# Layer 1's modulation: from matmul steps among the mixers' work to VectorE dot products among layer 0's MLP blocks

## Chip, cores and metric

One NeuronCore of a Trainium2 chip runs the whole program. TensorE (PE) multiplies matrices, VectorE (DVE) and ScalarE (ACT) work on 128 partitions of a tile, GpSimd (POOL) adds some squares here, and the queue of SyncE (SP) issues every load. Each engine takes its instructions strictly in the order in which they stand in its queue; semaphores let them wait for one another. The metric is the time of one execution in microseconds (us).

## Reference

Two transformer blocks run on 256 tokens of 1024 features, in fp32. Only the first block is touched. It has two layers, and in each the scale, shift and gate vectors ("modulation") of the token stream x and of a context stream ctx come from two conditioning vectors c and c_ctx:

```python
silu_c, silu_cc = jax.nn.silu(c), jax.nn.silu(c_ctx)
...
for l in range(DEPTH):                       # DEPTH = 2
    mx = jnp.split((silu_c @ w_mod[l] + b_mod[l])[:, None, :], N_MOD, axis=-1)   # w_mod[l]: 1024 x 6144
    mc = jnp.split(silu_cc @ w_mod[l] + b_mod[l], N_MOD, axis=-1)
    zx = modulate(rms_norm(x, norm1_g[l]), mx[0], mx[1]) @ w_in[l]
    ...                                      # mixer: latent attention, Fourier group, convolution
    x = x + mx[2] * mixer_rest(fx, gx, attn_x, l)
    hx = modulate(rms_norm(x, norm2_g[l]), mx[3], mx[4])
    x = x + mx[5] * channel_mlp(hx, l)       # relu(h @ w_mlp1)^2 @ w_mlp2, 1024 -> 4096 -> 1024
```

The same is done for ctx with mc in layer 0. For each layer the modulation is a 2 x 1024 by 1024 x 6144 product, kept on the chip as a tile `mod` of 128 partitions x 2 streams x 48 columns. Block 2's cross-attention reads keys and values of a memory of 256 tokens, whose products (`memory()`) depend on nothing else.

## The kernel before

Features lie on partitions, tokens along the free axis (n = 512 for both streams, 256 for x alone). An fp32 product is three passes over exact parts: `wsplit` (line 582) loads a 512 KB chunk of weights into a slot `raw` (four slots, line 577), ACT casts it to the high part `wh`, DVE subtracts to get the low part `wl` (three slots each), and 24 matmuls per output block of 128 features take high x high, high x low and low x high. PE is fed block after block; each output block of 128 x 512 is one PSUM bank `mm` and is read by DVE and ACT when it is finished.

The modulation is `modulation(l)` (line 727), a generator with 24 steps per layer. A step takes two `raw` chunks of w_mod, 16 matmul instructions into the PSUM tile `md`, a copy `mrow` on ACT, four short matmuls with a selection matrix, and a DVE add with the bias into `mod`. All steps of both layers are *filler*: `weave` (line 1425) interleaves the mixer's chains (values and keys, queries, attention, Fourier, convolution, the input projection) by a model of the engines and takes a filler step when no other product could go. Layer 0's mixer takes the rest of layer 0's steps and then steps of layer 1; layer 1's mixer alternates layer 1's remaining steps with chunks of `memory()` (line 850; 16 chunks of 24 matmuls, tile `ax<-hl`), and what is left of `memory()` runs after the mixer. The step order is fixed when the program is built, and a scheduler may still move instructions of one engine past each other before the queues are written.

After each mixer comes the output projection (`wo`, 8 blocks) with `resid` (line 824): DVE adds the gated block to x, ACT squares x for the norm, and DVE and ACT prepare the *early* operand x times scale (tile `hl<-x,s`), on which the first two blocks of the MLP start before the norm is known. Then the norm itself: ACT's `y`, DVE's `q`, `q`, `y` (`rsqrt`, line 697), and for 8 feature tiles x 2 streams DVE's `tmp<-x,s,y` and ACT's and DVE's two parts `hl<-tmp,mod`. The MLP (`mlp`, line 1270) is 32 `up` blocks (`ev_mlp`: `tmp<-mm`, `hid`) and 32 `down` blocks (`x<-mm,mod,x`), in quarters of 8. All loads go through SP's one queue in order.

Of the kernel before, what the change touches and what calls it, by code (L numbers as in the profile page):

```python
# [27 lines left out]
# ------------------------------------------------------------------ layouts  # L28


def pack_w(w, kt, mc):
    """[kt*128, M] -> [M/mc, 128, mc/128 * kt * 128]: chunks that load contiguously, output block by block."""
    m = w.shape[1]
    return np.ascontiguousarray(
        w.reshape(kt, P, m // mc, mc // P, P).transpose(2, 1, 3, 0, 4).reshape(m // mc, P, kt * mc)
    )


def cols(v):
    """A vector of n*128 -> [128, n]."""  # L40
    return v.reshape(-1, P).T


def feat(a):
    """[T, D] -> [128, D/128, T]."""
    return a.T.reshape(-1, P, a.shape[0]).transpose(1, 0, 2)
# [97 lines left out]
INS = "ckv kr g0 a0 cq0 cq1 g1 a1 zf0 zf1".split()  # order of the blocks of w_in  # L144


def layout(i):
    """All device arrays, laid out; and where each small vector lies."""
# [4 lines left out]
    a["mem"] = np.ascontiguousarray(feat(i["mem_2"][0]))  # L153
    for l in range(2):
        a[f"w_mod{l}"] = np.ascontiguousarray(
            i["w_mod"][l].reshape(KD, P, 3, 2, KD, P).transpose(2, 4, 1, 0, 3, 5)).reshape(24, P, 2048)
# [64 lines left out]
# ------------------------------------------------------------------ program  # L221


TICK = 10.24 / 3  # of the PE's activity monitor, in us


class Engine:
    """An engine whose instructions the model of the core notes as they are issued."""
# [13 lines left out]
class Pool:  # L242
    """A tile pool whose slots' reuse the model notes."""
# [19 lines left out]
class Core:  # L263
    """The core, with a model of when each engine gets to what has been issued, in us.

    It serves only to choose the order in which work that does not depend on each other is traced."""
# [3 lines left out]
    TAIL = {"pe": 0.19, "dve": 0.16, "act": 0.18, "pool": 0.2, "dma": 2.0}  # until others see an end  # L270

    def __init__(self, nc):
# [3 lines left out]
        self.columns = {}  # tick of the PE's activity monitor -> columns counted  # L276
        self.used = {}    # tile -> end of its last use
        self.seen = {}    # tile -> accesses: box, end, engine, whether written
        self.last = 0.0   # the latest end since it was set to 0
        self.gaps = {k: [] for k in self.clock}  # when an engine waits, which later work may use  # L280
# [5 lines left out]
    def box(ap):  # L286
        """The first and last partition and element that an access touches."""
# [4 lines left out]
    def product(self, start, name, n, rows, cols, f32):  # L292
        """How long a product takes: the PE runs at half its rate after a tick with too few columns."""
# [28 lines left out]
    def after(self, ap):  # L322
        """When what has been issued so far has written ap."""
# [7 lines left out]
    def cooling(self):  # L331
        """Whether the PE has too few columns in this tick so far to run at its full rate in the next."""
# [3 lines left out]
    def place(self, key, ready, held):  # L336
        """When an instruction starts that could at ready: in the first gap that holds it, or behind the last."""
# [47 lines left out]
class Chain:  # L385
    """Work that is traced in steps: a generator that stops before products that wait for other engines.

    It yields the tiles that the next product waits for, nothing if that is all of the step, or a chain that has to
    end first. A chain that is mostly the DVE's (dve) goes on when the DVE has nothing else."""
# [6 lines left out]
class Squares:  # L396
    """Sums of squares over the features of tiles that come one by one: all but the last are added up on the way."""
# [1981 lines left out]
```

## Time and profile before

| | |
|---|---|
| time, median of 3 runs | 1751.02 us (1748.15 to 1751.82) |
| profiled execution: first to last instruction | 1750.8 us, at a mean granted TensorE clock of 0.962 |
| busy: PE, DVE, ACT, POOL | 1667.3, 1158.8, 853.1, 81.1 us |
| PE's busy time on `md` | 89.85 us for 48 steps |
| HBM traffic | 142 GB/s on average |

The profiled execution's span lies 0.2 us below the median of the runs, so the sums further down are made against 1750.8 us and need no correction. All instructions are issued by one helper, so the profile's line is always L238 and the tiles tell what an instruction is. The stages on the profile's clock: layer 0's mixer to 254 us (its own modulation is done at 200), its output projection to 296, norm and MLP to 654, layer 1's mixer to 821, the rest of `memory()` to 850, then layer 1's output projection, its MLP and block 2.

### The profile page before, as it was taken

The page shows a single profiled execution, that of the slowest core. Times are in us where ns is not written, and L with a number is a line of the kernel's source. Part 1 is how long each engine was busy: PE and PEld are TensorE (multiplying, and loading weights), DVE is VectorE, ACT ScalarE, POOL GpSimd, SP SyncE. Part 2 cuts the span into 40 slices and gives each one's busy share as a digit, 9 for nine tenths or more (in the row PEclk, how much of TensorE's full clock was granted, in tenths as well). Part 3 has the DMA queues.
Part 4 walks back from the last instruction along what each step waited for, and adds up shares of the span by engine and source line. Part 5 has one row for each costly group of instructions (what it writes and reads, how often), then busy time and mean ns, then how long its engine had stood idle before and what let it go on. Part 6 is the DMA issues. An engine that isn't in the chain of part 4 may idle for free.

```text
span 1750.8 us, 29987 instructions
## 1 busy us (share of the span) xinstructions
PE 1667.3 (95%) x12072; PEld 1429.8 (82%) x12072; DVE 1158.8 (66%) x2155; ACT 853.1 (49%) x1485; POOL 81.1 (5%) x74
## 2 busy tenths in 40 slices
PE   5899999999999998999999998899999999999997
PEld 3666668788888886767999997797888899999997
DVE  4686547743444366884679667787853868788864
ACT  4426764441323245466564446542334746666643
POOL 0000001000000011000100001011000001010000
PEclk8989999999999998989999998999988999999999
DMA  8743562233333335752756564332211475345553
GB/s 276 236 150 126 180 205 85 85 97 96 96 97 96 115 98 168 238 168 70 223 150 185 184 187 149 106 105 66 67 61 49 137 250 192 112 154 192 167 164 105
DMA packets 69403, 248.94 MB, mean 142 GB/s; under 512 B 7696, under 2 KB 13072, under 8 KB 65424
## 3 DMA queue, kind: packets, MB, share of 16 engines
q1 hardware_dynamic: 69264, 247.03, 44.2%
q8 instruction: 95, 1.56, 0.4%
q14 instruction: 44, 0.36, 0.1%
HBM read 242.80 MB, written 4.19 MB: 141 GB/s over the span
## 4 chain that ended last, share of the span: by engine, by line
PE 83%; DVE 8%; DMA 4%; ACT 4%; issue 1%; POOL 0%; SPq 0%; DVEq 0%; ACTq 0%
PE mm L238 63%; PE ax L238 11%; PE md L238 3%; PE sc L238 3%; PE fx L238 3%; DVE wl L238 2%; DMA raw<-w_in 1%; ACT wh L238 1%; DMA raw<-w_mod 1%; DVE tmp L238 1%; DVE y L238 1%; ACT L238 1%; DVE hl L238 1%; DMA x<-xc 0%; DVE x L238 0%
## 5 line engine op out<-in xcount | busy, mean ns | idle before, releaser
L238 PE MATMUL mm<-hl,wh 128*128 128x256 f32 (+2 forms) x3856 | 867.5, 320 | 15.0 <-DVE rw_in L238 7.6
L238 PEld LDWEIGHTS mm<-hl,wh 128*128 128x128 f32 x3856 | 645.5, 194 | 76.1 <-issue 8.7
L238 ACT CAST wh<-raw 128x1024 fp32r<-128x1024 f32 (+1 forms) x353 | 360.8, 1024 | 558.1 <-PE mm L238 434.3
L238 PE MATMUL mm<-hl,wl 128*128 128x256 f32 (+1 forms) x1928 | 613.4, 319 | 3.9 <-DVE wl L238 3.8
L238 DVE TENSOR_TENSOR wl<-raw,wh 128x1024 fp32r<-128x1024 f32 (+1 forms) x353 | 422.3, 1198 | 223.9 <-ACT wh L238 221.8
L238 PEld LDWEIGHTS mm<-hl,wl 128*128 128x128 f32 x1928 | 372.8, 193 | 30.4 <-DVE wl L238 6.8
L238 PE MATMUL mm<-y,wh 128*128 128x256 f32 x928 | 176.5, 290 | 7.1 <-DVE early L238 2.6
L238 PEld LDWEIGHTS mm<-y,wh 128*128 128x128 f32 x928 | 147.7, 194 | 10.3 <-DVE early L238 3.0
L238 PE MATMUL mm<-y,wl 128*128 128x256 f32 x464 | 133.1, 287 | 0.0
L238 DVE SCALAR_TENSOR_TENSOR x<-mm,mod,x 128x256 f32<-128x256 f32 x120 | 54.3, 480 | 117.9 <-PE mm L238 117.8
L238 POOL TENSOR_TENSOR sq<-sq,sq 128x256 f32<-128x256 f32 (+1 forms) x48 | 59.9, 1249 | 899.7 <-ACT sq L238 899.4
L238 PEld LDWEIGHTS mm<-y,wl 128*128 128x128 f32 x464 | 89.7, 193 | 0.6 <-issue 0.5
L238 PE MATMUL md<-raw,cs 128*32 128x256 f32 x768 | 62.6, 424 | 20.0 <-DMA raw<-w_mod 11.4
L238 PE MATMUL mm<-hid,wh 128*128 128x512 f32 x256 | 80.7, 397 | 0.0
L238 DVE SCALAR_TENSOR_TENSOR acc<-u,vec,acc 128x512 f32<-128x512 f32 (+1 forms) x120 | 73.2, 614 | 2.2
L238 ACT ACT_TABLE_LOAD x49 | 62.9, 1283 | 4.7 <-DMA vec<-vec 3.6
L238 PEld LDWEIGHTS md<-raw,cs 128*32 128x32 f32 x768 | 20.4, 115 | 48.6 <-issue 11.4
L238 PEld LDWEIGHTS mm<-hid,wh 128*128 128x128 f32 x256 | 48.2, 188 | 11.7
L238 PE MATMUL mm<-hid,wl 128*128 128x512 f32 x128 | 50.7, 396 | 0.0
L238 DVE TENSOR_REDUCE mx<-sc 128x1 f32<-128x512 f32 (+1 forms) x56 | 32.1, 574 | 24.5 <-PE sc L238 24.1
L238 PE MATMUL sc<-k,hl 96*128 96x512 f32 (+1 forms) x144 | 46.0, 420 | 1.4 <-ACT prob L238 1.4
L238 ACT CAST hl<-tmp 128x256 fp32r<-128x256 f32 (+1 forms) x62 | 28.7, 470 | 28.0 <-DVE tmp L238 27.8
(377 smaller groups left out, 2089.6 us busy)
## 6 DMA issues: line engine op xcount, KB each, us to landing
raw<-w_mlp SPq DMA_DIRECT2D x128, 512.0 KB, 3.6
raw<-w_mod SPq DMA_DIRECT2D x96, 512.0 KB, 4.7
raw<-w_up SPq DMA_DIRECT2D x22, 1024.0 KB, 4.9
raw<-w_gate SPq DMA_DIRECT2D x24, 512.0 KB, 3.6
raw<-w_down SPq DMA_DIRECT2D x16, 704.0 KB, 4.1
raw<-w_in SPq DMA_DIRECT2D x20, 512.0 KB, 4.7
raw<-w_o SPq DMA_DIRECT2D x16, 512.0 KB, 4.0
raw<-w_rw SPq DMA_DIRECT2D x14, 512.0 KB, 3.6
```

Source lines behind the costliest of these rows:

```text
L238: return f(out, *args, **kw)
```

## The change

Layer 0's modulation stays as it was. Layer 1's leaves TensorE: `dots()` loads w_mod[1] transposed, 128 output features on the partitions and 1024 inputs along the free axis (48 loads of 512 KB), broadcasts c and c_ctx to all partitions once (`cb`, 1 MB, ACT applies silu), and takes for each of the 48 chunks two DVE instructions that multiply and sum over the free axis. One chunk is issued after each output block of layer 0's MLP. `need_mod` takes from the same generator, and layer 1's mixer has `memory()` alone for filler.

```diff
+        a["w_mod0"] = np.ascontiguousarray(
+            i["w_mod"][0].reshape(KD, P, 3, 2, KD, P).transpose(2, 4, 1, 0, 3, 5)).reshape(24, P, 2048)
+    a["w_mod1"] = np.ascontiguousarray(i["w_mod"][1].T).reshape(48, P, D)
+    a["ccrow"] = np.ascontiguousarray(np.stack([i["c"][0], i["c_ctx"]]).reshape(1, 2 * D))
...
+    def dots(self):
+        nc = self.nc
+        pool = self.tm.tp
+        cb = pool.tile([P, 2 * D], F32, name="cb")
+        nc.sync.dma_start(cb, self.a["ccrow"].partition_broadcast(P))
+        nc.scalar.activation(cb, cb, AF.Silu)
+        mod, bm = self.mods[1], self.v("b_mod1")
+        w = [self.raw(self.a["w_mod1"][0], D)]
+        for b in range(48):
+            yield
+            if b < 47:
+                w.append(self.raw(self.a["w_mod1"][b + 1], D))
+            for i in range(2):
+                t = pool.tile([P, D], F32, tag="dot", bufs=1, name=self.nm("dot"))
+                nc.vector.tensor_tensor_reduce(t, w[b], cb[:, i * D:i * D + D], 1.0, bm[:, b:b + 1], ALU.mult, ALU.add,
+                                               accum_out=mod[:, i, b:b + 1])
+            if b % 16 == 15:
+                self.mod_done[1] = b // 16 + 1
...
     def fillers(self):
-        for m in self.mod_gen:
-            yield from m
+        yield from self.mod_gen[0]
...
-            next(self.filler.gen)
+            next(self.dot if l else self.filler.gen)
...
-            def fill():
-                gens = [self.filler.gen, self.memory()]
...
-            filler = Chain(fill(), fill=True)
+            filler = Chain(self.memory(), fill=True)
...
             hid[m] = (hi, lo)
+            if l == 0:
+                next(self.dot, None)
...
+        if l == 0:
+            self.dot = self.dots()
+            next(self.dot)
         self.mark(f"L{l}.norm2")
...
+            def evac(m, ps):
+                add(m, ps)
+                if l == 0:
+                    next(self.dot, None)
```

The scheduler does not leave the dot products where the code issues them. On DVE, at the norm behind layer 0's output projection, the queue of before holds the last weight split, the last early operand (`x_97` is the last of the eight tiles of x), and then the norm's `q`, `q`, `y` and the scaled tiles:

```order
L238 TENSOR_TENSOR wl_2777<-raw_2774,wh_2776 128x1024
L238 SCALAR_TENSOR_TENSOR hl_2560<-x_97,s_115,hl_2560 128x256 x2
L238 SCALAR_TENSOR_TENSOR q_2592<-y_2591 128x512
L238 SCALAR_TENSOR_TENSOR q_2592<-ax_2588,q_2592 128x512
L238 SCALAR_TENSOR_TENSOR y_2591<-q_2592,y_2591 128x512
L238 SCALAR_TENSOR_TENSOR tmp_2598<-x_90,s_115,y_2591 128x256 x2
```

The same place now, where a dot product is a row `ISA dot_...` and the row `ISA mod_117 128x1` behind it writes its sum:

```order
L240 SCALAR_TENSOR_TENSOR hl_2391<-x_97,s_115,hl_2391 128x256 x2
L240 ISA dot_2753,mod_117<-raw_2708,cb,vec 128x1024
L240 ISA mod_117 128x1
L240 ISA dot_2755,mod_117<-raw_2708,cb,vec 128x1024
L240 ISA mod_117 128x1
L240 SCALAR_TENSOR_TENSOR q_2428<-y_2427 128x512
L240 ISA dot_2796,mod_117<-raw_2751,cb,vec 128x1024
L240 ISA mod_117 128x1
L240 SCALAR_TENSOR_TENSOR q_2428<-ax_2424,q_2428 128x512
L240 ISA dot_2798,mod_117<-raw_2751,cb,vec 128x1024
L240 ISA mod_117 128x1
L240 SCALAR_TENSOR_TENSOR y_2427<-q_2428,y_2427 128x512
```

Four dot products stand between the last early operand and `y`, and eight more stand in the output projection ahead of it: one in each of the blocks that write `x_91` to `x_94`, two in those of `x_95` and `x_96`. The chunks that they read come through the same four `raw` slots as the other weights, and of the w_mod1 chunks the fourth, fifth and sixth (`raw_2659`, `raw_2708`, `raw_2751`) lie in one slot, so each is loaded when the dot products of the one before it are done. In SP's queue of the changed kernel they stand between loads of w_mlp:

```order
L240 DMA cb<-ccrow 128x2048
L240 DMA raw_2321<-w_o 128x1024
L240 DMA raw_2410<-w_mod 128x1024
L240 DMA raw_2412<-w_mlp 128x1024
L240 DMA raw_2418<-w_mlp 128x1024
L240 DMA raw_2600<-w_mod 128x1024
L240 DMA raw_2616<-w_mod 128x1024
L240 DMA raw_2622<-w_mlp 128x1024
L240 DMA raw_2659<-w_mod 128x1024
L240 DMA raw_2665<-w_mlp 128x1024
L240 DMA raw_2671<-w_mlp 128x1024
L240 DMA raw_2708<-w_mod 128x1024
```

No such w_mod load stood there before.

On PE, at the start of layer 1's mixer, the queue of before goes from the last product of the shifts (`ax<-sh`) over a modulation step to the sums of the key-value norm (`ax_5256`), two more pieces of modulation, and the key-value products (`mm<-wkh,hl`):

```order
L238 MATMUL ax_5137<-sh_5134,wl_5035 128x2
L238 MATMUL md<-cst_a,mrow_5208 128x2 x2
L238 MATMUL ax_5256<-sq_5254,cst_a 128x512
L238 MATMUL md<-raw_5243,cs 32x256 x4
L238 MATMUL md<-raw_5323,cs 32x256 x4
L238 MATMUL md<-cst_a,mrow_5241 128x2 x2
L238 MATMUL md<-raw_5335,cs 32x256 x4
L238 MATMUL mm_5377<-wkh_5250,hl_5025 128x512
```

Now the sums of the memory's norm (`ax_5358`) stand ahead of those of the key-value norm (`ax_5403`), and a whole chunk of memory products (`ax_5554`, 24 matmuls) ahead of the key-value products (`mm_5454`):

```order
L240 MATMUL ax_5259<-sh_5256,wl_5157 128x2
L240 MATMUL ax_5358<-sq_5336,cst_a 128x256
L240 MATMUL ax_5358<-sq_5356,cst_a 128x256
L240 MATMUL ax_5403<-sq_5401,cst_a 128x512
L240 MATMUL ax_5554<-hl_5368,wh_5450 128x256 x2
L240 MATMUL ax_5554<-hl_5368,wl_5451 128x256
...
L240 MATMUL ax_5554<-hl_5389,wh_5450 128x256 x2
L240 MATMUL ax_5554<-hl_5389,wl_5451 128x256
L240 MATMUL mm_5454<-wkh_5397,hl_5147 128x512
```

All `md` rows are gone from here on; on DVE the memory's norm (8 x `mem<-mem,vec,y`, 8 x `hl<-mem`) stands ahead of the second `q` of the key-value norm.

## Rows read from the trace of the kernel before

**Rows 1.** The page: span, and busy time of each engine.

```profile
span 1750.8 us, 29987 instructions
PE 1667.3 (95%) x12072; PEld 1429.8 (82%) x12072; DVE 1158.8 (66%) x2155; ACT 853.1 (49%) x1485; POOL 81.1 (5%) x74
```

**Rows 2.** Stretches, all engines: PE, PEld, DVE, ACT, POOL busy (count), clock, DMA, GB/s.

```profile
200.00:254.00 54.00, 53.20 (x466) 36.38 (x462) 26.00 (x68) 38.01 (x95) 0.00 (x0) 1.00 0.68 222
325.00:654.00 329.00, 328.69 (x1437) 269.89 (x1437) 153.67 (x201) 107.33 (x144) 9.09 (x8) 1.00 0.33 101
688.00:821.00 133.00, 123.04 (x897) 96.72 (x897) 97.16 (x212) 81.10 (x160) 3.12 (x3) 0.92 0.49 164
821.00:850.00 29.00, 29.00 (x243) 28.98 (x242) 12.16 (x14) 12.08 (x17) 0.00 (x0) 1.00 0.66 203
```

**Rows 3.** The same view for tile md alone: PE, PEld, DVE, ACT.

```profile
200.00:254.00 54.00, 16.59 (x204) 9.39 (x204) 1.64 (x10) 3.69 (x10) 1.00 0.68 222
654.00:688.00 34.00, 6.61 (x60) 2.98 (x60) 0.48 (x3) 1.11 (x3) 0.86 0.46 146
688.00:800.00 112.00, 20.44 (x216) 11.31 (x216) 1.95 (x12) 4.10 (x11) 0.91 0.56 188
```

**Rows 4.** DVE groups by shape: count, busy us, mean ns, idle before.

```profile
L238 DVE TENSOR_TENSOR wl<-raw,wh 128x1024 fp32r<-128x1024 f32 x321 | 393.8, 1228 | 196.4 <-ACT wh L238 194.3 <-ACT hl L238 1.2
...
L238 DVE SCALAR_TENSOR_TENSOR acc<-u,vec,acc 128x512 f32<-128x512 f32 x60 | 44.4, 749 | 1.2
...
L238 DVE TENSOR_TENSOR_SCAN s_z<-s_d,s_z 128x512 f32<-128x512 f32 x16 | 20.5, 1283 | 0.4
```

**Rows 5.** Loads of w_mlp: KB each, median us from issue to landing.

```profile
raw<-w_mlp SPq DMA_DIRECT2D x128, 512.0 KB, 3.6
```

**Rows 6.** Timeline of DVE, one output-projection block: start, length, idle before.

```profile
284.20 0.88 DVE L238 SCALAR_TENSOR_TENSOR x<-mm,mod,x 128x256 f32<-128x256 f32 x2 [1.53 <-PE mm L238]
285.06 1.23 DVE L238 TENSOR_TENSOR wl<-raw,wh 128x1024 fp32r<-128x1024 f32 x1
286.20 1.91 DVE L238 SCALAR_TENSOR_TENSOR hl<-x,s,hl 128x256 fp32r<-128x256 f32 x2
```

**Rows 7.** Timeline of DVE, layer 0's second norm.

```profile
301.66 0.69 DVE L238 SCALAR_TENSOR_TENSOR q<-y 128x512 f32<-128x512 f32 x1 [3.71 <-ACT y L238]
...
303.84 6.03 DVE L238 SCALAR_TENSOR_TENSOR tmp<-x,s,y 128x256 f32<-128x256 f32 x15
309.78 4.84 DVE L238 SCALAR_TENSOR_TENSOR hl<-tmp,mod,hl 128x256 fp32r<-128x256 f32 x12
```

**Rows 8.** Timeline of PE there.

```profile
316.27 0.50 PE L238 MATMUL mm<-hl,wl 128*128 128x512 f32 x1 [0.63 <-DVE wl L238]
```

**Rows 9.** Timeline of DVE, one up block.

```profile
342.64 1.23 DVE L238 TENSOR_TENSOR wl<-raw,wh 128x1024 fp32r<-128x1024 f32 x1 [2.01 <-ACT wh L238]
343.79 0.68 DVE L238 SCALAR_TENSOR_TENSOR tmp<-mm,tmp 128x512 f32<-128x512 f32 x1
345.15 0.69 DVE L238 TENSOR_TENSOR hid<-tmp,hid 128x512 fp32r<-128x512 f32 x1 [0.69 <-ACT hid L238]
348.08 1.23 DVE L238 TENSOR_TENSOR wl<-raw,wh 128x1024 fp32r<-128x1024 f32 x1 [2.24 <-ACT wh L238]
```

**Rows 10.** Timeline of PE, start of layer 1's mixer.

```profile
685.46 1.08 PE L238 MATMUL md<-raw,cs 128*32 128x256 f32 x8 [2.82 <-DVE mod L238]
688.05 0.79 PE L238 MATMUL mm<-wkh,hl 128*128 128x512 f32 x1 [1.51 <-ACT hl L238]
```

**Rows 11.** Timelines of POOL and of DVE there, the memory's norm.

```profile
690.13 1.38 POOL L238 TENSOR_TENSOR sq<-sq,sq 128x256 f32<-128x256 f32 x1 [0.31 <-ACT sq L238]
...
695.62 3.26 DVE L238 SCALAR_TENSOR_TENSOR mem<-mem,vec,y 128x256 f32<-128x256 f32 x8
698.80 1.43 DVE L238 TENSOR_TENSOR hl<-mem,hl 128x256 fp32r<-128x256 f32 x4
```

**Rows 12.** Stretches of 5 us there, columns as in group 2.

```profile
685.00:690.00 5.00, 3.03 (x13) 1.77 (x14) 2.96 (x5) 4.60 (x10) 4.47 (x5) 0.51 0.84 262
```

More of the change, by code (lines that the diff above doesn't have):

```diff
@@ L153, in layout @@
     a["mem"] = np.ascontiguousarray(feat(i["mem_2"][0]))
+    a["w_mod0"] = np.ascontiguousarray(
+        i["w_mod"][0].reshape(KD, P, 3, 2, KD, P).transpose(2, 4, 1, 0, 3, 5)).reshape(24, P, 2048)
+    a["w_mod1"] = np.ascontiguousarray(i["w_mod"][1].T).reshape(48, P, D)
+    a["ccrow"] = np.ascontiguousarray(np.stack([i["c"][0], i["c_ctx"]]).reshape(1, 2 * D))
     for l in range(2):
-        a[f"w_mod{l}"] = np.ascontiguousarray(
-            i["w_mod"][l].reshape(KD, P, 3, 2, KD, P).transpose(2, 4, 1, 0, 3, 5)).reshape(24, P, 2048)
         w = i["w_in"][l]
@@ L1234, in mixer @@
         if l:
-            def fill():
-                gens = [self.filler.gen, self.memory()]
-                while gens:
-                    for g in list(gens):
-                        y = next(g, self)
-                        if y is self:
-                            gens.remove(g)
-                        else:
-                            yield y
-            filler = Chain(fill(), fill=True)
+            filler = Chain(self.memory(), fill=True)
         self.weave(*chains, Chain(conv(), dve=True), Chain(ins), filler)
@@ L1315, in down @@
         def down(qd, *late):
-            self.linear(a[f"w_mlp2{l}"], KD, P, [hid[8 * qd + k] for k in range(8)], n,
-                        self.resid(mod, 5, streams, *late), range(8 * qd, 8 * qd + 8))
+            add = self.resid(mod, 5, streams, *late)
+            def evac(m, ps):
+                add(m, ps)
+                if l == 0:
+                    next(self.dot, None)
+            self.linear(a[f"w_mlp2{l}"], KD, P, [hid[8 * qd + k] for k in range(8)], n, evac, range(8 * qd, 8 * qd + 8))
         for qd in range(4):
@@ L1354, in block1 @@
             self.mods = [self.c1.tile([P, 2, 48], F32, name=f"mod{l}") for l in range(2)]
-            self.mod_gen = [self.modulation(l) for l in range(2)]
+            self.mod_gen = [self.modulation(0)]
             self.mod_done = [0, 0]
```

## The prediction

> **What bounds the kernel now.** First the page: PE is busy 1667 of 1751 us, DVE 1159 [rows 1]. Such a kernel gets shorter by work taken from PE, but only in stretches where PE is what is waited for. So next the stretches that the change touches [rows 2]. In layer 0's mixer, once its own modulation is done (200 to 254), PE has 0.8 us of idle time and ACT is busy 38 of 54 us. In the MLP (325 to 654) PE idles 0.3 of 329 us and DVE is busy 154: DVE has room, and nothing that delays PE would be hidden. In layer 1's mixer PE idles 10 of 133 us behind 688, and behind 821 it works on what is left of the memory without a gap. Then the modulation's own share of PE in these stretches [rows 3]: 16.6, 6.6 and 20.4 us. Of the 16.6, about 15% is the end of layer 0's steps, which stay; 9.5 steps, 14 us, are layer 1's.
>
> **Layer 0's mixer.** These steps are filler: they ran when no other product could go, so without them PE will partly wait. PE would be left with 53.2 - 14 = 39 us of work in the 54, ACT, without its copies (3.7 us [rows 3]), with 34. Neither can be packed without gaps, as the softmax goes back and forth between PE, DVE and ACT. The gain lies between 0 (every step stood in a wait) and 14 (none did). I take 8, a stage of 46 us with PE 85% busy, a little nearer to the work that remains, since three other chains run beside attention.
>
> **The output projection and the norm behind it.** Here the order shows twelve of the 96 dot products. Their price is not in the trace. The nearest row is the weight split, also fp32, both sources in SBUF, over the same 128x1024: 1.23 us [rows 4]. The sum is read out by a second, tiny instruction; DVE's tiny `mod` adds took 0.16 us each (1.64 for 10 [rows 3]). I take 1.35 us for both, a little overlapped; below, 1.2; above, the price of an operation that carries a running value, the scan: 1.28 us for 512 elements [rows 4], 2.4 to 2.5 us for 1024.
>
> In a block of the output projection DVE waits 1.53 us for PE [rows 6]. One dot product per block fits there; two make it 2.7 - 1.5 = 1.2 us late. To this come the loads. A chunk lands 3.6 us after its issue [rows 5], and is issued when a slot falls free. Take the blocks at 284.20 [rows 6] and every 5.44 us before and behind it, so that x is written at 262.4 (`x_91`) to 295.1 (`x_97`). Chunk 1 gets its slot when that first block's weight split ends, at 264.4, and lands at 268.1; DVE comes to it at 266.3 and waits. Chunk 2 waits likewise for the split two blocks later. Going through the blocks in this manner I get DVE late by 1.7, 1.4, 3.0, 2.7, 3.8 and 4.8 us, so that the update of `x_97` ends at 300.7 in place of 296.0. PE does not feel this by itself: split weights are two blocks ahead.
>
> Then the chain of loads in one slot: chunk 4's dot products end at 299.5, chunk 5 lands at 303.2, its two end at 305.9, the first `q` follows to 306.6; chunk 6, issued at 305.9, lands at 309.6; then dot, `q`, dot, `y`, with 0.69 us for `q` [rows 7]: 309.6 + 1.35 + 0.7 + 1.35 + 0.7 = 313.7. Before, `y` was done when the scaled tiles began, at 303.84 [rows 7]: 9.9 us late. Behind it stand 15 scaled tiles (6.0 us) and then the first low part, which PE's third product on the norm needs; it was done at 310.2 and will be at 320.2. There was no reserve: PE's wait at 316.27 [rows 8] is for a weight split behind this same DVE chain. So PE loses nearly all of the 9.9 us and a little at the next two splits, behind which two more dot products stand: 10.5 us. If DVE is not late at `x_97` it is 5; if the loads take 1 us more and do not overlap, 14. A pause also costs clock: in the 5 us in which PE was busy 3.0 the granted clock was 0.51 [rows 12], the lower of its two levels (1.2 of 2.4 GHz). I add 1 us (0 to 3). Sum: +11.5 us (5 to 17).
>
> The rest of `dots()` I count at nothing. The load of `cb` (1 MB, twice a chunk, so some 7 us) and its silu are first read by the first dot product, which waits for its chunk anyway; if that did not cover them, they would cost up to 4 us at that same place, and the chain of loads behind it would move by as much.
>
> **The MLP.** An up block has the split (1.15 us from start to start), `tmp` (0.68) and `hid` (0.69) on DVE, 2.52 us of every 5.44 [rows 9]. With two dot products it is 5.22: 96%, still inside. A down block has two updates (0.86 [rows 6]) and the split, 4.7 with the dots. The splits keep a reserve of one to two blocks, and DMA goes from 101 GB/s [rows 2] by one 512 KB chunk more per block to about 200, against 262 in another stretch [rows 12]. I take 0 (0 to 10).
>
> **Layer 1's mixer.** Behind 688 the steps' 20.4 us [rows 3] go away. `memory()` stays as filler, 29 us of it were run bare at the end [rows 2], and it can take the steps' places: I count all 20.4. But ahead of 688 the order has changed. PE's sums for the key-value norm now stand behind those of the memory's norm, and a whole memory chunk stands ahead of the key-value products. Before, the memory's last square was added on POOL until 691.5, its scaled tiles ran from 695.6 to 698.9 on DVE, and eight low parts followed, four of them in 1.43 us [rows 11], while the key-value products had begun at 688.05 [rows 10]. The memory's loads still go out behind weights of this stage, so I leave its norm where it was, within 3 us: low parts done at 703. The key-value norm's second `q`, `y`, scaling and split add 3 us (0.7 each): products at 706, 18 us later, in which PE has done one useful chunk, 24 x 29.0/243 = 2.9 us [rows 2]. The 6.6 us of steps ahead of 688 filled waits (2.82 and 1.51 us beside them [rows 10]) and gain nothing. Net: -20.4 + 18 - 2.9 = -5.3 us (-20 to +3).
>
> **The sum.** -8 + 11.5 + 0 - 5.3 = -1.8 us on 1750.8: 1749.0 us; the span lies 0.2 us under the median of the runs, which changes nothing. A change below 0.2% (3.5 us) cannot be told from none here, so I forecast no measurable change, out of three terms of both signs that are each larger than that.
>
> **Rivals.** *The memory is ready in time.* With layer 1's w_mod loads gone from SP's queue, the memory's tiles could land and be squared up to 12 us earlier, and its norm would not hold the key-value products. For it: an emptier queue. Against it: the loads stand behind weight chunks whose slots come free in the same norm. Then layer 1 gains all of its 20: 1749 - 15 = 1734 us.
>
> *DVE becomes the bound of the up blocks*, a slower kernel. The margin there is 5.44 - 5.22 = 0.22 us. From 1.46 us per dot product on, each further 0.1 us costs 0.2 us in each up block with dots; 84 dots, two to a block, make some 26 up and 16 down blocks. For it: the price of the dot is an estimate, and a DVE that leaves the norm 10 us late cannot catch up at 96%. Against it: PE was set back by the same 10 us. At 1.6 us: 26 x 0.28 = 7, and 12 x 0.25 = 3 more in the norm: 1759 us.
>
> *The dot product runs at half rate*, like the scan. Then an up block needs 2.5 + 5.0 = 7.5 us of DVE, a down block 7.0, against 5.44: 26 x 2.1 + 16 x 1.6 = 80, and 12 x 1.1 = 13 in the norm: 1842 us. Against it: the fused `acc<-u,vec,acc`, which reads two SBUF tiles, takes 749 ns for 512 elements [rows 4], not the scan's 1283. The Trainium skill (Vector Engine (DVE) Microarchitecture Reference, section "Points that are easy to get wrong") says that the fused scalar-tensor-tensor form with two SBUF sources that are not bf16 runs at half throughput, with no port left to read the accumulator back; by that rule the time would be this rival's. The `acc` rows have such sources and do not show the halving, but they write no accumulator, so they do not settle it for a dot product.
>
> **Chances.** The forecast's case, within about 8 us of its sum (1741 to 1757), 0.5: of these 0.17 faster by over 0.2%, 0.21 within, 0.12 slower. The memory in time 0.22, faster. DVE as the bound of the up blocks, or the norm's chain at its upper end, 0.20, slower. Half rate 0.08, slower. Together faster 0.39, same 0.21, slower 0.40. The range 1731 to 1766 takes in the two middle rivals and leaves out half rate and the outer ends.
>
> **What the new profile would show.** Layer 0's output projection would begin at about 246 us. Between the last `x<-mm` and the end of `y` in the norm behind it would lie 13 us (7.9 before), with two waits for w_mod loads around the first `q`, and PE would have a gap of 8 to 10 us with a lower clock behind it. In the up blocks a dot product would take 1.2 to 1.4 us, and PE would stay without gaps. In layer 1 the key-value products would begin 18 us later, counted from the last down block, than before. The prediction is wrong if dots take over 1.46 us, if the norm's `y` is under 6 us late, or if the key-value products do not wait for the memory chunk.

## The result, and the profile after

The changed kernel takes 1763.5 us (median of 5 runs, 1761.3 to 1766.6) against 1748.6 us before on the same chip; the ratio is estimated at 1.0079, 95% interval 1.0055 to 1.0104. It is slower by 0.8%, where I forecast 1749.0 us and no measurable change. The profiled execution's span is 1763.5 us. The page of the changed kernel begins with it:

```profile
span 1763.5 us, 29176 instructions
PE 1642.7 (93%) x11592; PEld 1412.3 (80%) x11592; DVE 1265.1 (72%) x2323; ACT 848.4 (48%) x1463; POOL 80.5 (5%) x74
```

PE's busy time fell by 24.6 us against [rows 1], and the span still grew by 12.7 us. The busy totals can't tell why; the length of each stage can. The table takes stages from the starts of DVE's `q<-y`, `x<-mm,mod,x`, the end of `y<-q,y` and PE's first `mm<-wkh`, in the profiled execution of each kernel (the experiments, told below, are listed with it so that all stand side by side). Columns: start to the query norm's `q`; to layer 0's first `x` of `wo`; to the end of the norm's `y`; to the first down update of its MLP; to the last one; to layer 1's key-value products; to layer 1's first `x` of `wo`; all the rest (layer 1's MLP and block 2, whose code no kernel here changes but for a number of temporary buffers); span. All in us.

| kernel | q | x | y | down 1 | last down | kv | wo 1 | rest | span |
|---|---|---|---|---|---|---|---|---|---|
| before | 176.2 | 80.8 | 46.8 | 92.5 | 258.9 | 32.9 | 164.9 | 897.8 | 1750.8 |
| **after** | 178.3 | 80.0 | 56.6 | 95.4 | 268.7 | 42.6 | 141.7 | 900.2 | 1763.5 |
| late | 176.9 | 80.0 | 46.8 | 107.5 | 262.6 | 42.7 | 140.8 | 906.4 | 1763.7 |
| ntmp4late | 178.1 | 79.9 | 46.8 | 104.3 | 263.8 | 43.7 | 139.6 | 906.3 | 1762.5 |
| own2 | 178.0 | 79.4 | 58.0 | 92.8 | 258.8 | 42.6 | 138.9 | 902.0 | 1750.5 |
| own2late | 176.4 | 80.0 | 46.8 | 91.2 | 258.3 | 42.7 | 140.8 | 901.3 | 1737.5 |
| kv | 177.4 | 79.5 | 57.6 | 95.6 | 269.5 | 27.5 | 152.1 | 902.6 | 1761.8 |
| own2latekv | 175.6 | 79.8 | 46.8 | 91.2 | 258.3 | 27.5 | 153.3 | 896.8 | 1729.3 |
| own2latekv2 | 176.2 | 77.3 | 46.8 | 91.2 | 258.3 | 37.3 | 151.7 | 899.3 | 1738.1 |
| warm | 176.7 | 85.7 | 57.2 | 93.8 | 267.2 | 42.5 | 137.0 | 899.0 | 1759.1 |
| hyb (9 steps) | 175.9 | 80.4 | 46.8 | 91.2 | 258.3 | 42.6 | 140.5 | 891.1 | 1726.8 |
| hyb6 | 176.8 | 79.3 | 46.8 | 91.9 | 257.6 | 42.7 | 138.4 | 895.8 | 1729.3 |
| hyb4 | 178.8 | 75.7 | 46.9 | 91.9 | 257.6 | 42.7 | 138.9 | 906.3 | 1738.8 |
| hyb2 | 176.6 | 78.5 | 46.8 | 91.2 | 258.3 | 44.5 | 141.0 | 916.5 | 1753.4 |
| hybkv | 177.0 | 79.3 | 46.8 | 91.2 | 258.3 | 27.5 | 155.5 | 907.9 | 1743.5 |

From before to after: +2.1, -0.8, +9.8, +2.9, +9.8, +9.7, -23.2, +2.4 us, which is the +12.7.

**Layer 0's mixer** is no shorter. Two stretches of it after, all engines, columns as in [rows 2]:

```profile
200.00:254.00 54.00, 47.05 (x270) 31.86 (x270) 24.52 (x63) 35.11 (x89) 0.00 (x0) 0.91 0.11 35
200.00:220.00 20.00, 17.62 (x79) 11.70 (x80) 9.66 (x26) 11.98 (x31) 0.00 (x0) 0.74 0.16 60
```

The loads of the steps are gone (35 GB/s in place of the 222 of [rows 2]) and PE ran 270 matmuls in place of 466, but it was busy 47 us with them, 8 more than the 39 left by the steps, and idle for the other 7. The granted clock was 0.91 in the 54 us and 0.74 in their first 20; before it was 1.00 [rows 2].

**The price of a dot product.** DVE's groups by shape, columns as in [rows 4]:

```profile
L240 DVE CUSTOM_DVE_ANT_0 dot<-raw,cb,vec 128x1024 f32<-128x1024 f32 x96 | 125.8, 1311 | 55.9 <-DMA raw<-w_mod 55.8
L240 DVE DVE_READ_ACCUMULATOR2_ANT mod<- 128x1 f32 x96 | 7.9, 82 | 0.0
```

The second group is the instruction that reads the sum out. The idle time says more than the price: DVE waited 55.8 us for w_mod chunks to land.

**The norm behind the output projection.** From the chain of work that ended last between 300 and 325 us, the pieces around the norm (start, length, what):

```profile
300.77 4.36 DMA raw<-w_mod
305.13 0.03 issue
305.16 1.29 DVE dot L240
...
306.49 1.28 DVE dot L240
...
307.81 3.27 DMA raw<-w_mod
...
311.21 1.28 DVE dot L240
...
312.51 0.60 DVE q L240
313.11 1.19 DVE dot L240
...
314.31 0.61 DVE y L240
...
314.95 4.51 DVE tmp L240 x12
```

Two loads and four dot products stand in the chain ahead of `y`, as predicted from the order. The waits of PE from 312 to 325 us (total, times, longest) are what PE paid for it:

```profile
PE mm L240 <- ACT hl L240: 4.1, 1, 4.1
PE mm L240 <- DVE hl L240: 2.1, 1, 2.1
PE mm L240 <- ACT wh L240: 1.7, 1, 1.7
```

**The MLP** is where the forecast of nothing fails. The waits of PE and of DVE from 330 to 660 us:

```profile
PE mm L240 <- DVE wl L240: 8.3, 12, 1.7
```

```profile
DVE dot L240 <- DMA raw<-w_mod: 47.0, 30, 3.0
```

DVE is not the bound there: it stood waiting 47 us in 30 dot products, and 12 times PE waited for a split behind one of them. The timeline shows the loop, first the issues on SP's queue, then DVE (start, length, engine, line, operation, wait):

```profile
461.38 0.33 SPq L240 DMA_DIRECT2D raw<-w_mod  x1
463.19 0.33 SPq L240 DMA_DIRECT2D raw<-w_mlp  x1
467.56 0.33 SPq L240 DMA_DIRECT2D raw<-w_mod  x1
```

```profile
460.13 1.22 DVE L240 TENSOR_TENSOR wl<-raw,wh 128x1024 fp32r<-128x1024 f32 x1
...
465.10 1.28 DVE L240 CUSTOM_DVE_ANT_0 dot<-raw,cb,vec 128x1024 f32<-128x1024 f32 x1 [1.34 <-DMA raw<-w_mod]
466.31 0.08 DVE L240 DVE_READ_ACCUMULATOR2_ANT mod<- 128x1 f32 x1
466.31 1.22 DVE L240 TENSOR_TENSOR wl<-raw,wh 128x1024 fp32r<-128x1024 f32 x1
```

The w_mod chunk gets the slot that the split ending at 461.35 leaves. It lands at 465.10, its first dot ends after 1.21 us, and the next split, which frees a slot for the next chunk, follows: the next issue is at 467.56. From issue to issue 6.2 us: 3.7 of load, 1.2 of dot, 1.2 of split. A block of PE's takes 5.44. The 8.3 us of waits are most of the 9.8 us that this stage grew by.

**Layer 1's mixer.** The longest wait of PE from 690 to 723 us, and the piece of POOL's timeline that it waits for:

```profile
PE ax L240 <- POOL sq L240: 10.5, 1, 10.5
```

```profile
703.08 5.07 POOL L240 TENSOR_TENSOR sq<-sq,sq 128x256 f32<-128x256 f32 x6 [26.70 <-ACT sq L240]
```

PE's sums for the memory's norm wait for POOL's last square, and the key-value products stand behind them, as the order said. The memory's low parts follow on DVE, and are done at 718.73:

```profile
715.97 2.76 DVE L240 TENSOR_TENSOR hl<-mem,hl 128x256 fp32r<-128x256 f32 x8
```

### The profile page after: what moved, and what is told of

It is laid out like the page before. It is cut to its first block, busy times and chain, and to the rows that moved or that the text cites. A ratio compares the mean times of both kernels' runs of the same rounds, so it can differ in the third digit from the quotient of the medians.

```text
span 1763.5 us, 29176 instructions
## 1 busy us (share of the span) xinstructions
PE 1642.7 (93%) x11592; PEld 1412.3 (80%) x11592; DVE 1265.1 (72%) x2323; ACT 848.4 (48%) x1463; POOL 80.5 (5%) x74
## 4 chain that ended last, share of the span: by engine, by line
PE 64%; DVE 15%; DMA 10%; ACT 6%; issue 5%; SPq 0%; POOL 0%; DVEq 0%; ACTq 0%; POOLq 0%
PE mm L240 48%; PE ax L240 10%; DMA raw<-w_mod 8%; DVE wl L240 4%; PE fx L240 3%; PE sc L240 3%; DVE dot L240 2%; PE md L240 1%; ACT wh L240 1%; DVE tmp L240 1%; ACT prob L240 1%; ACT L240 1%; DVE hl L240 1%; DMA raw<-w_in 1%; DVE s_z L240 1%
## 5 line engine op out<-in xcount | busy, mean ns | idle before, releaser
L240 PE MATMUL mm<-hl,wh 128*128 128x256 f32 (+2 forms) x3856 | 864.8, 319 | 24.6 <-DVE rw_in L240 7.6
L240 PE MATMUL mm<-hl,wl 128*128 128x256 f32 (+1 forms) x1928 | 612.5, 318 | 11.5 <-DVE wl L240 11.2
L240 ACT CAST wh<-raw 128x1024 fp32r<-128x1024 f32 (+1 forms) x353 | 360.9, 1024 | 498.2 <-PE mm L240 363.2
L240 PEld LDWEIGHTS mm<-hl,wl 128*128 128x128 f32 x1928 | 370.7, 192 | 44.1 <-DVE wl L240 20.4
L240 DVE CUSTOM_DVE_ANT_0 dot<-raw,cb,vec 128x1024 f32<-128x1024 f32 x96 | 125.8, 1311 | 55.9 <-DMA raw<-w_mod 55.8
L240 PE MATMUL md<-raw,cs 128*32 128x256 f32 x384 | 32.7, 437 | 16.6 <-ACT warm L240 8.4
```

What stands on the lines that cost most here:

```text
L240: return f(out, *args, **kw)
```

## Experiments

All comparisons are by stage first. The column "rest" moves from 891 to 916 us among kernels whose code is the same there (hyb and hyb2), so a total by itself says little of an edit that is worth less than that. The stages come from one profiled execution of each kernel.

### Does the norm lose by its place, and the MLP by its slots?

My theory was that the MLP loses by the w_mod chunks sharing the four `raw` slots with the weights, and the norm by the dot products that stand in its chain. Rival: DVE is simply too full in both, and any dots there cost PE time. **late** makes the dot products only from the first up block on (`later` lets the load of `cb` wait for a tile of that block); **own2** gives the chunks two slots of their own and takes four temporaries away to make room; **own2late** does both; **ntmp4late** is `late` with the fewer temporaries alone.

```diff
 # late
+        self.later(cb, after)
...
+                if m == 0:
+                    self.dot = self.dots(t)
...
-        if l == 0:
-            self.dot = self.dots()
-            next(self.dot)
 # own2
-        w = [self.raw(self.a["w_mod1"][0], D)]
+        def chunk(b):
+            t = pool.tile([P, D], F32, tag="wdot", bufs=2, name=self.nm("wdot"))
+            nc.sync.dma_start(t, self.a["w_mod1"][b])
+            return t
+        w = [chunk(0)]
...
-            self.tm.ntmp, self.tm.nt = 8, T if l else 512
+            self.tm.ntmp, self.tm.nt = 4, T if l else 512
```

> The dot products can start only when the first output block of the MLP is through (the load of the broadcast vectors waits for it), so none stands in the output projection or in the norm. Theory (the norm's chain lost what the trace after shows, some 12 us of idle PE and lower clock there): the output projection and norm go as before, about 11 us less, 1752 us; the waits for chunk loads in the up blocks stay. Rival (DVE is full, and the twelve dot products only move to up blocks that have no room for them): under 4 us less, 1760 us or more.

Measured: 1766.5 us, ratio 1.0101 (1.0077 to 1.0125). The norm is back at 46.8 us, but the stretch behind it is 12.1 us longer than after, so the rival's number came out, though not for its reason. The first chunks take shared slots while `cb` is not there yet, so weights cannot load; ACT's longest waits from 325 to 640 us are for the weights, PE waits once for ACT, and its granted clock is 0.74 from 330 to 350 us:

```profile
ACT wh L240 <- DMA raw<-w_mlp: 69.2, 20, 10.1
```

```profile
PE mm L240 <- ACT wh L240: 6.9, 1, 6.9
```

So the loss moved; it did not go. This too is an effect of the shared slots, by a second way: own2late, below, starts as late and does not have it.

> The control of the own slots: late start and only four slots for plain activations, but the chunks in the shared slots. Theory (the own slots made the 29 us between the late start and the late start with own slots): as the late start, 1764 us within 4. Rival (fewer activation slots change the order on DVE and that did it): 1745 us or less.

Measured: 1765.6 us, ratio 1.0083 (1.0054 to 1.0113), stages within 3.2 us of `late`. The number of temporaries is not what helps below.

> Two slots of their own for the chunks, but no late start: dot products stand again in the output projection and between the norm's q, q and y. Theory (the slots cause the MLP's loss, and in the norm the loads' part of the lateness, two to three waits of 1 to 3 us; the dot products themselves in DVE's queue keep some 5 us of it): 1737 + 5 = 1742 us, y of the norm 5 to 7 us late. Rival (the DVE queue alone makes the norm's loss): y 10 us late or more, 1749 us.

Measured: 1749.5 us, ratio 1.0001 (0.998 to 1.0021). The MLP takes 258.8 us, as before, and PE no longer waits in it; DVE's waits for chunks fall from 55.8 to 2.3 us. But the norm still takes 58.0 us. With the chunks there in time the scheduler sets six dot products between the last update of `x` and `y`, where there were four, and one more behind `y`; the six in DVE's timeline there:

```profile
302.79 1.27 DVE L240 CUSTOM_DVE_ANT_0 dot<-wdot,cb,vec 128x1024 f32<-128x1024 f32 x1
...
305.92 1.27 DVE L240 CUSTOM_DVE_ANT_0 dot<-wdot,cb,vec 128x1024 f32<-128x1024 f32 x1
...
307.70 1.28 DVE L240 CUSTOM_DVE_ANT_0 dot<-wdot,cb,vec 128x1024 f32<-128x1024 f32 x1 [0.50 <-DMA wdot<-w_mod]
...
309.03 1.28 DVE L240 CUSTOM_DVE_ANT_0 dot<-wdot,cb,vec 128x1024 f32<-128x1024 f32 x1
...
310.24 0.69 DVE L240 SCALAR_TENSOR_TENSOR q<-y 128x512 f32<-128x512 f32 x1
311.74 1.28 DVE L240 CUSTOM_DVE_ANT_0 dot<-wdot,cb,vec 128x1024 f32<-128x1024 f32 x1 [0.81 <-DMA wdot<-w_mod]
...
313.56 1.28 DVE L240 CUSTOM_DVE_ANT_0 dot<-wdot,cb,vec 128x1024 f32<-128x1024 f32 x1
...
314.76 0.69 DVE L240 SCALAR_TENSOR_TENSOR y<-q,y 128x512 f32<-128x512 f32 x1
```

So in the norm the rival is right: with or without load waits, DVE's queue there costs 10 to 11 us.

> As the late start, and the chunks of w_mod1 have two slots of their own (the plain activations give up four of their eight slots for them). Theory (a slot loop: a chunk's load waits for the slot of the weight split that stands right behind the dot product before it, 3.7 + 1.2 + 1.1 = 6.1 us per block against 5.44): the 47 us of DVE waiting for chunk loads go to under 5, PE's 8.3 us of waits for split weights in the MLP to under 2, and the time is 8 us below the late start alone, 1744 us. Rival (DVE is full at 96% and late anyway): PE's waits stay, within 2 us of the late start.

Measured: 1737.5 us, ratio 0.993 (0.9906 to 0.9954). Norm 46.8, MLP 258.3 us. The stretch 325 to 654 us:

```profile
325.00:654.00 329.00, 329.00 (x1438) 269.92 (x1437) 265.59 (x395) 109.70 (x146) 9.28 (x8) 1.00 0.55 176
```

DVE does 265.6 us of work there, 112 more than before [rows 2], and PE has not one gap. The rival falls for the MLP: dots that have slots of their own cost nothing there, dots in the shared slots do.

### Layer 1: what is the early norm worth?

**kv** holds the whole memory filler back until the key-value chain is queued; **own2latekv** does it on top of own2late, **own2latekv2** holds only what comes behind the memory's squares, **hybkv** does it on top of hyb (below).

```diff
-            filler = Chain(self.memory(), fill=True)
+            def held():
+                yield E["kv"]
+                yield from self.memory()
+            filler = Chain(held(), fill=True)
```

> The kernel after, with the memory's products held back in layer 1's mixer until the key-value products are issued. Theory (the key-value sums wait 10.5 us for the memory's squares because they stand behind them on TensorE): that wait goes, the key-value products begin 33 to 35 us behind the last down block in place of 42.5, and of the 9 us some 6 are kept: 1757 us. Rival (there is no other work at that place, and the memory's chunks are needed as cover for later waits): the wait comes back elsewhere in the mixer, 1762 to 1766 us.

Measured: 1761.0 us, ratio 1.0062 (1.0037 to 1.0086). The products come after 27.5 us, 15.1 earlier than after, and 10.4 us of it is lost again before the output projection. Of these PE's gaps are 3.3 us (14.9 against 11.6); the other 7.1 are busy time, in which the memory chunk of 2.9 us that now comes behind the products has its part and a granted clock of 0.92 against 0.95 another. Net -4.7 us, between the theory and the rival.

> Own slots and late start, and the memory held back in layer 1's mixer until the key-value products are issued. Theory (the gains add up: holding the memory back kept 4.7 of 15 us in layer 1): 1733 us. Rival (with the DVE and the queue less loaded the memory's chunks were no longer in the way): 1737 us as without it.

Measured: 1736.9 us, ratio 0.9922 (0.9891 to 0.9953). Layer 1's mixer takes 27.5 + 153.3 = 180.8 us against own2late's 183.5. The total is the rival's; its six runs fall into two groups, three from 1730.5 to 1731.8 us and three from 1742.0 to 1742.7, and the profiled one is of the first.

> As the kernel before in this list, but the memory's tiles are loaded and squared at the start and only its sums and products wait for the key-value products. Theory (what holding it back lost again, some 10 us behind the key-value products, was that its first chunk came too late to fill waits): 1728 to 1731 us. Rival (the loss behind them is the order of the remaining chains, not the missing filler): 1733 us, equal to the one before.

Measured: 1742.6 us, ratio 0.996 (0.994 to 0.998); 37.3 + 151.7 = 189.0 us. Neither forecast came: splitting the memory's squares from the rest is worse than holding all or nothing.

> The mixed version with nine steps, and the memory held back until the key-value products. If that keeps its 4.7 us here: 1725 us. If the gain is lost again behind the key-value products, as it was in part before: 1730 us, no difference.

Measured: 1741.3 us, ratio 0.9946 (0.9924 to 0.9968); 183.0 us against hyb's 183.1; the total missed both forecasts by the rest of the program (907.9 us against hyb's 891.1). The wait for POOL's square is real, but to remove it moves the wait: worth 0 to 5 us, not its 10.

### Layer 0's mixer: where did 14 us of PE work go?

Theory "chain": the softmax's way between PE, DVE and ACT sets the length, and the steps filled its gaps. Theory "clock": without the steps PE's granted clock falls, and what is left takes longer. **warm** fills with ten groups of eight matmuls on a constant (work that computes nothing). **hyb** is own2late with nine of layer 1's 24 steps left in layer 0's filler, and dots for the other 30 chunks; **hyb6**, **hyb4** and **hyb2** keep six, four and two steps.

```diff
 # warm, in fillers()
+        for i in range(10):
+            ps = self.mdp[:, i % 2, :]
+            for k in range(KD):
+                ...
+                self.nc.tensor.matmul(ps[32 * g:32 * g + 32, :], self.cs[:, k, :], self.cst["a"][:, 0:T], ...)
+            yield []
 # hyb, on top of own2late
         yield from self.mod_gen[0]
+        yield from self.modulation(1, 9)
...
-        for b in range(48):
+        todo = [b for b in range(16, 48) if b not in (16, 24)]
+        for j, b in enumerate(todo):
```

> The kernel after, with ten groups of eight matmuls on constants (no loads, result unused) as filler in layer 0's mixer once layer 0's modulation is through: what the removed steps did for TensorE's activity, without their work. Theory A (removing the steps gained nothing there because the rest is a serial chain over PE, ACT and DVE): output projection at 255 us as now, total within 3 us of 1763. Theory B (the stage became 8 us shorter in work, but the granted clock fell to 0.74 from 200 to 220 us and took it back): the clock stays at 1.0, the output projection begins 4 us earlier or more, 1759 us. If the groups stand in the way, it begins later by up to 5 us.

Measured: 1760.9 us, ratio 1.007 (1.0041 to 1.01). The stage got 5.7 us longer than after. The groups ran bunched and in the way (185 matmuls from 200 to 220 us, after 79), so it settles nothing on the clock.

> Own slots and late start, but nine steps of layer 1's modulation (18 of the 48 chunks) run on TensorE in layer 0's mixer again, as before the change; dot products take the other 30. Theory (these steps stood wholly in waits or in time that a lower clock takes otherwise, and the 18 chunks' dot products are hidden in the MLP): the output projection begins at 254 to 256 us, total 1737 us within 3. Rival (they cost there what they take, as the constant groups did): 5 us or more later, 1743 us.

Measured: 1730.1 us, ratio 0.9887 (0.9865 to 0.9909): the best version timed, ahead of both kernels. The nine steps cost nothing: 80.4 us, where none gave 80.0. The total is below both forecasts, which the last section of experiments comes back to. The two stretches, columns as above:

```profile
200.00:254.00 54.00, 52.05 (x437) 35.54 (x433) 26.57 (x68) 37.97 (x94) 0.00 (x0) 1.00 0.61 206
325.00:654.00 329.00, 329.00 (x1438) 269.90 (x1437) 223.85 (x322) 110.36 (x147) 9.28 (x8) 1.00 0.47 150
```

> As the mixed version, with four steps of layer 1's modulation in layer 0's mixer in place of nine. Theory (the length of that stage is a chain through softmax, and steps only fill its waits): from the query norm at 176 us to the output projection 80 us within 1, with 5 to 7 us of idle time on PE between the 2.1 of nine steps and the 8.7 of none; total as with nine, 1730 us within 4. Rival (nine steps and none agree by chance, work added against clock lost): 3 us or more shorter or longer.

Measured, one run: 1740.5 us. The stage took 75.7 us, but began 2 to 3 us later than in the others; its end, the first `x` of `wo`, lies at 254.5 us (before 257.0, own2late 256.4, hyb 256.3). The clock was 1.00 in every slice of 10 us from 176 to 256 us, PE's gaps 8.5 us. The stage is 4.3 us shorter than the theory had it, the rival's case, and this looked like the clock theory, so two more counts of steps were run.

> As hyb4, but with two steps of layer 1's modulation left among layer 0's mixers (4 of the 48 tiles) and 44 chunks as dot products, each started in its up block from a pool of its own. The stage from the query norm to the first x of layer 0's wo took 80.0 us with no step, 75.7 with four and 80.4 with nine. Clock theory (it takes little TensorE work in the gaps to keep the granted clock at full speed, and what there is costs its own 1.55 us a step): the clock stays near 1.00 in that stage and it takes 72.5 to 74 us. Rival, chain (the gaps belong to the softmax chain and its order, not to the clock; the 75.7 is an order that happened to be good): 76 to 80 us, with 8 to 10 us of TensorE waits. If two steps are too little to keep the clock: slices at 0.75 to 0.95, and 78 to 80 us. The MLP of layer 0 stays at 258 to 259 us.

Measured, one run: 1755.1 us; stage 78.5, its end at 255.1 us. Two steps did not keep the clock up, the third case of the expectation, and the length lies in its range. Two slices of 10 us, of own2late and then of this kernel (all engines, then the clock):

```profile
206.00:216.00 10.00, 8.75 (x37) 5.36 (x36) 4.70 (x10) 5.31 (x12) 0.00 (x0) 0.74 0.00 0
226.00:236.00 10.00, 7.32 (x44) 4.20 (x44) 6.74 (x14) 7.64 (x21) 0.00 (x0) 1.00 0.17 52
```

```profile
206.00:216.00 10.00, 9.18 (x38) 6.50 (x37) 6.04 (x13) 6.51 (x14) 0.00 (x0) 0.72 0.52 181
226.00:236.00 10.00, 8.69 (x40) 4.94 (x41) 5.07 (x13) 7.32 (x18) 0.00 (x0) 0.91 0.16 52
```

> As hyb4, with six steps in the fillers and 36 chunks as dot products. Clock theory: the clock is at 1.00 as with four, and two more steps cost 2 x 1.55 us: 78 to 79.5 us from the query norm to the first x of wo. Rival, chain: the two steps lie in gaps that are there anyway (7.8 us with four steps, 2.1 with nine), so the stage stays at 75.5 to 76.5 us and the gaps shrink to about 5. MLP of layer 0 at 258 to 259 us.

Measured, one run: 1731.1 us; stage 79.3, its end at 256.1 us, PE's gaps 7.6 us, the clock 1.00 but for 0.93 and 0.90 from 226 to 246 us. The length is in the clock theory's range, the clock is not what it wanted. With 0, 2, 4, 6 and 9 steps the stage takes 80.0, 78.5, 75.7, 79.3 and 80.4 us: from four steps on it grows by 0.9 us a step, where the clock theory wanted 1.55, and with fewer than four it grows too, at a lower clock. Counted by its end, at 256.4, 255.1, 254.5, 256.1 and 256.3 us, which leaves out that hyb4 began late, there is next to no slope. With one execution of each this does not decide between the theories. What does hold is that nine steps cost nothing there against none. Clock and waits are both seen; the same 80 us before and in own2late, which has no steps:

```profile
176.00:256.00 80.00, 76.84 (x608) 51.92 (x601) 39.03 (x95) 56.30 (x131) 0.00 (x0) 0.96 0.62 202
```

```profile
176.00:256.00 80.00, 69.15 (x411) 46.15 (x404) 37.72 (x86) 53.84 (x121) 0.00 (x0) 0.89 0.22 74
```

PE's busy time falls by 7.7 us and not by the 14 of the steps, and its gaps grow by 7.7. The other 6.3 us went into slower work; the clock's fall from 0.96 to 0.89 would make some 5 us of them, an estimate (0.07 of 69 us). Whether the stage would be shorter with no steps at a clock of 1.00 was not reached by any run; the shortest end seen, at full clock throughout, is 2.5 us ahead of before's.

### Why the totals scatter

hyb2 equals own2late to within 1 us up to 836 us and is 16 us longer in all. Two stretches of block 2, of hyb2 and then of hyb:

```profile
1236.00:1336.00 100.00, 100.00 (x819) 79.08 (x817) 51.95 (x107) 41.72 (x71) 2.35 (x4) 0.81 0.18 56
1336.00:1436.00 100.00, 96.19 (x685) 86.18 (x686) 61.96 (x116) 53.37 (x78) 0.00 (x0) 0.86 0.47 152
```

```profile
1236.00:1336.00 100.00, 100.00 (x813) 79.90 (x812) 49.37 (x106) 42.18 (x78) 2.35 (x4) 0.85 0.18 52
1336.00:1436.00 100.00, 94.42 (x759) 90.82 (x758) 75.94 (x139) 61.53 (x96) 0.00 (x0) 1.00 0.60 191
```

The granted clock differs (0.86 against 1.00 in the second row). In PE's queue the order of block 2's mixer differs too, as the scheduler places it anew in each kernel. Which of the two brings the other was not tried, and neither need be the edit's doing: runs of one and the same kernel differ too (before 1737.0 to 1757.8 us in 22 runs on that chip, hyb 1727.7 to 1734.9 in 6), and hyb2 was run once. For hyb this means: 17 us of its gain, up to layer 1's output projection at 835.7 us (853.0 before), come with the edit and return in hyb2, hyb4 and hyb6 (836.9, 832.5, 833.5); the further 7 us in the rest do not.

## Why the prediction was wrong, step by step

The sum was 14.5 us too low: 7.2 in layer 0's mixer, 1.2 in the norm, 9.8 in the MLP, 2.1 ahead of the query norm and 2.4 in the rest, less 8.2 in layer 1. Two terms failed: the 8 us taken off layer 0's mixer and the 0 for the MLP. The range of 1731 to 1766 held the result only by luck, since without the 8.2 us of layer 1 it would have been 1771.7. None of the three signs of being wrong that I named came; all three looked at other terms.

- **"Layer 0's mixer ... I take 8": wrong, it gained 0.8.** I counted busy time taken from a PE with 0.8 us of gaps as if half of it had to come back. The bound of 0 came out, and only in part for its reason, "every step stood in a wait". Of the 14 us, 7.7 came back as PE's waits in own2late, whose mixer has no steps either. The other 6.3 came back as slower work, a term that the sum did not have for this stage: the granted clock, 1.00 with the steps from 200 to 254 us, fell to 0.74 in places without them. Whether the stage would have been shorter had the clock stayed up is open.
- **"Output projection and norm, +11.5": right.** The two stretches together lost 12.7 us. The last update of `x` ended at 301.9 (predicted 300.7), `y` at 314.9 (313.7), in a run that had entered the stage 1.3 us later. (The walk takes 3.7 us for a load in place of the 3.6 of [rows 5]; that is 0.1 us each.) Two loads stood around the first `q`; PE's gaps were 8.8 us from 258 to 330, and the clock was 0.81 from 300 to 325. But the chain of loads was not a necessary part: with most of it gone (own2; two waits of 0.50 and 0.81 us stay), more dots slid in and the loss stayed.
- **"The MLP ... I take 0 (0 to 10)": wrong, it lost 9.8.** I compared DVE's work, 5.22, with PE's block, 5.44, and trusted to the reserve of splits. The work was right, as own2late's stretch without a gap shows. The step that failed is that nothing but DVE's work could set the pace: I did not follow the chain of slot, load, dot, split and slot that I had written down for the norm one paragraph earlier: 6.2 us. own2 takes the chunks out of that loop, and the 9.8 us are gone; its fewer temporaries are not the cause (ntmp4late).
- **The price of a dot: right.** 1.21 us from start to the read of its sum and 0.08 for the read, 1.3 for both against 1.35. The half-rate rival falls, on the measured time: 1024 elements at a mean of 1311 ns, in step with 748 for 512 in `acc`. The Trainium skill (Vector Engine (DVE) Microarchitecture Reference, section "Points that are easy to get wrong") has the scalar-tensor-tensor form with two SBUF sources that are not bf16 at half throughput. The trace does not tell whether a dot product, CUSTOM_DVE_ANT_0 by name, is of that form; if it is, the trace disagrees, with two fp32 sources in SBUF and an accumulator written.
- **"DVE becomes the bound of the up blocks", 1759 us:** nearest in time and place, wrong in cause. It needed dots over 1.46 us; they took 1.3, and DVE idled for loads, 47 us of it.
- **"Layer 1: -20.4 + 18 - 2.9 = -5.3": mechanism right, one size off; it gained 13.5.** Behind the products the gain was 23.2 us, against 23.3 predicted. The delay of the products was 9.7 us and not 18; that it comes from the memory standing ahead shows in kv, where they come 15.1 us earlier. The step that failed is "I leave its norm where it was, within 3 us": the memory's low parts were done 39.7 us behind the last down update where I had them at 48. The first of its eight loads went out 1.5 us earlier in that count and the last 4.9, since all were issued within 3.8 us where it took 7.2 before; they landed in a median of 3.5 us and not 5.8, and POOL's adds ended 7 us earlier (29.1 us behind the update, 36.3 before [rows 11]). So the rival "the memory is ready in time" was half true.
- **The parts not in the sum:** 2.1 us ahead of the query norm and 2.4 in the rest. Among all kernels these vary by 3 and by 25 us, so no cause in the change is shown for them.

## What to carry to other kernels

Before moving work onto an engine with room, follow each operand's slot around once: issue, landing, its reader, and whoever has to run before the next issue; if that loop is longer than the block, it stalls however much room the engine has, and slots of its own cured it here. A stretch in which filler runs and PE never idles need not be bound by PE: the filler may stand in waits, and is then free where it stands. Where a scheduler places the whole program anew, compare stages before totals: here stages that no edit touches differed by up to 25 us between single executions, more than the edit was worth.

## What the runs showed of the hardware

A DVE instruction with both its inputs in SBUF that starts during a POOL add takes longer by nearly what the add still has to run. Three of the 96 dot products began within an add of squares and took 2.16, 2.32 and 2.32 us; the median of the 92 that met none is 1.28 and their longest 1.29, and the one during which an add began took 1.27. One of them, DVE's timeline and then POOL's:

```profile
272.79 2.32 DVE L240 CUSTOM_DVE_ANT_0 dot<-raw,cb,vec 128x1024 f32<-128x1024 f32 x1
```

```profile
272.56 1.46 POOL L240 TENSOR_TENSOR sq<-sq,sq 128x512 f32<-128x512 f32 x1 [5.33 <-ACT sq L240]
```

The add ended at 274.02, 1.23 us into the dot, which took 1.04 us more than its usual time. The Trainium skill ("SBUF — State Buffer", section "SBUF: two separate sides") says that an operation of VectorE with two SBUF inputs and one of GpSimd that reads SBUF lock one another out for a whole instruction; the rows agree roughly, the dot's excess being 0.2 us under the rest of the add. An early operand `hl<-x,s,hl` that began at 868.34, 0.78 us into an add of 1.46, took 0.49 us more than usual, again 0.2 under the rest of the add. With one input in PSUM no delay shows: `x<-mm,x` began at 1490.98, 1.08 us into an add of 1.75, and took its usual 0.41.

The collisions are not new, and so they cost the change nothing. In the output projection six adds meet a DVE instruction in either kernel. Before, it is each time the early operand `hl<-x,s,hl`, which takes 1.51 us where the others take 0.47; both are in the 1.91 us of [rows 6]. After, it is two early operands, the three dots and one weight split (2.30 us at 289.68).
